# Expert stage of a two-block transformer: one gather for two experts, later transposes, one product for the remainders of gate and up

## The chip, the core and the metric

The kernel runs on one core of a Trainium2 chip. Its time is the device time of one execution in microseconds (us), the median over runs. A core has a matrix engine (TensorE; PE for its products, PEld for its weight loads), a vector engine (VectorE, DVE), an activation engine (ScalarE, ACT), GpSimd (POOL) and SyncE (SP), which here only issues DMAs of weights. Each engine works through its own queue in order and waits on semaphores for the others. Products go to PSUM, which has eight banks of 512 float32 columns; VectorE and ScalarE copy them from there.

## The reference, cut to what matters

The model has two blocks. The first is a convolution layer with a dense feed-forward, then an attention layer with a mixture of experts; the second has two more layers of other kinds. The change touches the mixture of experts alone: 256 tokens of width 1024, eight experts with a hidden width FF of 2816, and every token goes to its two best experts.

```python
logits = (h @ router_w + router_b).astype(jnp.float32)
top_vals, top_idx = lax.top_k(logits, TOP_K)
top_p = jax.nn.softmax(top_vals, axis=-1)
gates = jnp.sum(jax.nn.one_hot(top_idx, N_EXPERTS, dtype=jnp.float32) * top_p[..., None], axis=-2)
out = jnp.zeros_like(h)
for e in range(N_EXPERTS):
    out = out + gates[..., e:e + 1] * swiglu(h, w_gate[e], w_up[e], w_down[e])
```

Here swiglu(h, g, u, d) is (silu(h @ g) * (h @ u)) @ d. All inputs are float32, and the weights of one expert are 3 x 1024 x 2816 numbers, 34.6 MB.

## The kernel before, in words

Products in near float32 precision are made of three: each operand is split into a high part, rounded to the type float32r, and the rest as a low part, and `mm3` (L178) multiplies high by high, high by low and low by high into the same bank. A weight unit is 128 partitions by 1024 numbers, 512 KB. `wraw` (L129) loads it by a DMA on SyncE's queue into a raw buffer: six buffers "raw", and in the expert stage six more, "xraw", which two of five units use. `wload` (L140) splits it: ScalarE writes hi (L152), then VectorE writes lo as raw minus hi (L154). There are four hi and four lo buffers. So a unit goes through SyncE, ScalarE, VectorE and TensorE in turn.

The stage is `moe` (L853); eight PSUM banks are shared out as four "mm" (gate and up), two "sm" (gathers, transposes and the sums at the end) and two "py" (down). `experts` (L847) goes through the eight experts. Only the tokens that chose an expert are computed, up to 128 in a pass; a second pass, behind an If at the end, is for experts with more.

`gather` (L743) brings an expert's tokens together. VectorE makes a one-hot matrix of tokens by slots (L753, two instructions of 128 columns). TensorE multiplies the high and the low part of the tokens with it (L763): 8 chunks of the width, 2 parts, 2 token blocks, so 32 products of 128 columns. Four chunks fill a bank, and the four banks are copied into exh by ScalarE (L768) and exl by VectorE (L766). Then TensorE transposes the one-hot (L774) and gathers each slot's gate (L776), and VectorE copies both (oT, gs). exh, exl and oh have two buffers. The gather of expert 0 comes ahead of all experts; that of expert e + 1 is written into expert e, between its last panel and its down product (`ahead`, L823).

`expert` (L783) goes through four panels of the hidden width: 1024, 1024, 512 and 256 columns. In each panel `proj` (L793) makes the gate product (xh and xl stationary, the weights moving, at most 512 columns a product), ScalarE applies silu into h (L809), `proj` makes the up product, VectorE multiplies it into h (L814), TensorE transposes h in blocks of 128 (L819, four to a bank), ScalarE copies them as hTh (L821) and VectorE the rest as hTl (L822). The panel of 256 has 24 products of 256 columns for gate and 24 for up. The down product then has 22 units of 6 products (py). At the end ScalarE and VectorE scale it by the gate (yh, yl), TensorE brings it back to token order with oT (L842, L843), and VectorE adds it to xt (L844).

The program's text is not quite the order of the queues: when the kernel is built, a scheduler orders each engine's instructions by their place in the text and by when it estimates their inputs to be there. So products of the next panel can stand ahead of transposes that are written before them.

Of the kernel before, what the change touches and what calls it, by code (L numbers as in the profile page):

```python
# [7 lines left out]
F32 = mybir.dt.float32  # L8
F32R = mybir.dt.float32r
# [3 lines left out]
ALU = mybir.AluOpType  # L13
# [3 lines left out]
P = 128  # L17
# [25 lines left out]
class K:  # L43
# [21 lines left out]
    def psum(self, name, **cfg):  # L65
        """PSUM of a phase: banks a tag; each stream of work has its own"""
        assert sum(cfg.values()) <= 8
        self.cfg = dict(cfg)
        return self.tc.tile_pool(name=name, bufs=1, space=PSUM, reuse_waits="tile")
# [25 lines left out]
    def load_vecs(self, psp, groups, eng):  # L95
        """per-feature vectors as columns: V[:, vidx[name] + i] holds elements 128 i .. 128 i + 127"""
# [32 lines left out]
    def wraw(self, src, a, b, pool=None):  # L129
# [7 lines left out]
        self.nc.sync.dma_start(raw[:, :a * b].rearrange("p (a b) -> p a b", a=a), src)  # L137
        return raw
# [18 lines left out]
    def hold(self, ins, n):  # L157
        """the low halves of the next n units wait their turn behind ins"""
        self.held = [ins, n]
# [24 lines left out]
    def ws(self, psp, W, c0, ncol, xs, kc, kper, evac, tag="mm", pre=None):  # L184
        """out fm: chunk pairs [P, 2, 256] per bank; evac(ps, i) for pair i"""
# [16 lines left out]
    def ws32(self, psp, W, c0s, x, evac):  # L202
        """256 columns from each of c0s on, out fm, in whole float32 products; evac(pss, h) when the half h is done"""
# [15 lines left out]
    def tsteps(self, psp, W, c0, ncol, xs, kc, kper, evac, tag="mm", tail=1, pre=None, k0=0):  # L219
        """a step a group of units; out tm: [P tok, ncol] per token block; evac(ps, blk); block 0 is ahead by the last tail units; chunks from k0  # L220
        on first"""
# [21 lines left out]
    def narrow(self, pool, psp, W, c0, n, xs, fn, tag):  # L243
        """n < 128 columns of xs @ W: fn(ps, blk) with ps [P tok, n]"""
# [10 lines left out]
    def grouped(self, units, n, tail):  # L255
        """single units, the last tail of the n in one group"""
# [9 lines left out]
    def newton(self, pool, v, n, tag="nw", y=None):  # L266
        """(v) ** -0.5 on a [P, n] tile"""
# [18 lines left out]
    def bcast_rows(self, ps, col, b):  # L286
        """ps[:, P] <- col ([P,1], one value a token) laid along the free dim of all partitions"""
        self.nc.tensor.matmul(ps, col.to_broadcast([P, P]), self.ident, start=True, stop=True, skip_group_check=True)

    def stats(self, pool, psp, xf, kc=KC, div=D):  # L290
        """rstd of an fm tile: columns [P, 2] and rows [P, 256]"""
# [42 lines left out]
    def to_fm(self, psp, xt, fn, tag="tr"):  # L334
        """xt tm [P, 2, 1024]; fn(ps, c) with ps [P, 2, 256] holding chunks c, c+1"""
# [17 lines left out]
    def conv(self, psp, filler):  # L353
        nc, tc, I = self.nc, self.tc, self.I
        W = I["conv_w_in"][0]
        with tc.tile_pool(name="cv", bufs=1, reuse_waits="tile") as pool:
# [31 lines left out]
            for j in range(4):  # L388
# [14 lines left out]
                if j == 0:  # L403
                    # whole float32 products where the splits would be waited for
# [37 lines left out]
                else:  # L442
                    # squares of the first three pairs about their own mean m0, which leaves them a sum of zero
# [18 lines left out]
                    # columns: sum and sum of squares about m0  # L462
# [9 lines left out]
            # layer norm over channels: (x - m0 - d) * r, d and r by columns, then by rows  # L472
# [68 lines left out]
    def softcols(self, pool, lg):  # L541
        """log(1 + exp(-|lg|))"""
# [7 lines left out]
    def fattn(self, psp, xf, ox):  # L550
        """x2 fm -> x3 tm (written into ox [P, 2, 1024])"""
        nc, tc, I = self.nc, self.tc, self.I
        with tc.tile_pool(name="fa", bufs=1, reuse_waits="tile") as pool:
# [14 lines left out]
            # cumulative log sigmoid F, with its sign as softmax takes it, laid along the keys of every head  # L568
# [12 lines left out]
            # columns: queries 0..127 on keys 0..127, queries 128..255 on keys 0..255; -(F_q - F_k) up to F_q, which  # L581
            # is the same for all the keys of a row and leaves the softmax as it is
# [70 lines left out]
    def router(self, psp, xt, st):  # L653
        """xt: x3 tm [P, 2, D]; fills st with h3 hi / lo (tm), one-hot slots and gates"""
        nc, tc, I = self.nc, self.tc, self.I
        pers = st["pool"]
        with tc.tile_pool(name="rt", bufs=1, reuse_waits="tile") as pool:
# [43 lines left out]
            for i in range(2):  # L701
# [5 lines left out]
                if i == 0:  # L707
                    # the chosen one leaves the range of any finite logit
# [961 lines left out]
```

## Time and profile before

| | |
|---|---|
| median of 3 runs | 2069.69 us (2066.9 to 2072.44) |
| the profiled execution, first to last instruction | 2068.7 us |
| TensorE products busy | 2008.7 us (97%), 12347 products |
| VectorE busy | 1501.9 us (73%) |
| ScalarE busy | 1259.1 us (61%) |
| mean granted TensorE clock | 0.987 |
| DMA, share of 16 engines (SyncE's queue) | 64.2%, 451.07 MB |

The profile is one execution, taken by the hardware. Busy time of TensorE is modelled at the ends of products, which overlap; two starts in the timeline give the real distance. L with a number is the line of the kernel that made an instruction, and an arrow out<-in gives its tiles. Idle time of an engine is put down to what ended it.

### The profile page before, as it was taken

Reading aid. Unit: us, or ns where it says so; the run is one execution under the profiler, and the core shown is the slowest. Engines: PE = TensorE matmul, PEld = TensorE weight load, DVE = VectorE, ACT = ScalarE, POOL = GpSimd, SP = SyncE. Lnnn points to the kernel's source line nnn. Section 1 sums busy time; section 2 is a strip of 40 time slices with the busy share of each in tenths; the row PEclk is TensorE's granted clock in tenths of the full one; section 3 lists DMA queues with packets and bytes.
Section 4 is the critical chain, followed back from the end, with each engine's and each line's share of the span. In section 5 each row is a group of like instructions: output and inputs, shape, how many; then the busy total and the mean of one; then the engine's idle time right before and its main releaser. Section 6 shows DMA issues by size and latency. Waiting matters only on the chain. (4 is left out here: it accounts for less than half of the span.)

```text
span 2068.7 us, 32399 instructions
## 1 busy us (share of the span) xinstructions
PE 2008.7 (97%) x12347; PEld 1771.2 (86%) x12347; DVE 1501.9 (73%) x2089; ACT 1259.1 (61%) x1705; POOL 123.7 (6%) x236
## 2 busy tenths in 40 slices
PE   7989999999999999999999999899999999999998
PEld 7879999988888888888888888799889988888986
DVE  5976664656889898898988888776256646657644
ACT  5654444554878786777777777665444534655543
POOL 7530000100000000000000000010000000110000
PEclk9989999999999999999999999999999999999999
DMA  5325655635999898999898999543126654345552
GB/s 188 97 61 169 184 184 164 215 112 185 331 331 368 319 371 299 352 332 358 327 360 324 364 330 353 201 146 110 32 82 184 184 189 144 95 133 162 185 178 97
DMA packets 218322, 455.08 MB, mean 220 GB/s; under 512 B 17865, under 2 KB 109186, under 8 KB 218160
## 3 DMA queue, kind: packets, MB, share of 16 engines
q1 hardware_dynamic: 215536, 451.07, 64.2%
q8 instruction: 98, 1.61, 0.3%
q10 hardware_dynamic: 2112, 1.64, 0.3%
q14 instruction: 64, 0.52, 0.1%
q0 software_dynamic: 512, 0.24, 0.0%
HBM read 451.83 MB, written 1.06 MB: 219 GB/s over the span
## 5 line engine op out<-in xcount | busy, mean ns | idle before, releaser
L154 DVE TENSOR_TENSOR lo<-raw,hi 128x1024 fp32r<-128x1024 f32 x633 | 764.8, 1220 | 306.6 <-ACT hi L152 301.9
L152 ACT ACTIVATE hi<-raw 128x1024 fp32r<-128x1024 f32 x633 | 665.1, 1057 | 491.4 <-PE mm L181 248.2
L180 PE MATMUL mm<-xs,hi 128*128 128x256 f32 (+1 forms) x1488 | 427.0, 287 | 6.1 <-ACT xs L497 3.0
L181 PE MATMUL mm<-xs,hi 128*128 128x256 f32 (+1 forms) x1488 | 426.8, 287 | 3.1 <-DVE xs L327 3.1
L182 PE MATMUL mm<-xs,lo 128*128 128x256 f32 (+1 forms) x1488 | 426.6, 287 | 1.8 <-DVE lo L154 1.8
L180 PEld LDWEIGHTS mm<-xs,hi 128*128 128x128 f32 (+1 forms) x1488 | 286.9, 193 | 8.7 <-issue 4.2
L181 PEld LDWEIGHTS mm<-xs,hi 128*128 128x128 f32 (+1 forms) x1488 | 286.8, 193 | 5.3 <-DVE xs L327 4.0
L182 PEld LDWEIGHTS mm<-xs,lo 128*128 128x128 f32 (+1 forms) x1488 | 286.3, 193 | 5.2 <-issue 2.4
L181 PE MATMUL mm<-lo,exh 128*128 128x512 f32 (+1 forms) x768 | 288.5, 376 | 0.3
L182 PE MATMUL mm<-hi,exl 128*128 128x512 f32 (+1 forms) x768 | 286.7, 373 | 0.0
L180 PE MATMUL mm<-hi,exh 128*128 128x512 f32 (+1 forms) x768 | 278.0, 373 | 0.0
L154 DVE TENSOR_TENSOR lo<-xraw,hi 128x1024 fp32r<-128x1024 f32 x211 | 254.3, 1221 | 25.0 <-ACT hi L152 21.1
L152 ACT ACTIVATE hi<-xraw 128x1024 fp32r<-128x1024 f32 x211 | 221.9, 1060 | 56.7 <-PE py L182 28.4
L181 PEld LDWEIGHTS mm<-lo,exh 128*128 128x128 f32 x768 | 144.5, 188 | 29.3 <-DVE lo L154 2.7
L180 PEld LDWEIGHTS mm<-hi,exh 128*128 128x128 f32 x768 | 144.6, 188 | 25.2
L182 PEld LDWEIGHTS mm<-hi,exl 128*128 128x128 f32 x768 | 144.6, 188 | 23.2
L182 PE MATMUL py<-hi,hTl 128*128 128x512 f32 x352 | 140.5, 399 | 0.0
L181 PE MATMUL py<-lo,hTh 128*128 128x512 f32 x352 | 140.1, 398 | 0.0
L180 PE MATMUL py<-hi,hTh 128*128 128x512 f32 x352 | 137.6, 400 | 0.0
L182 PE MATMUL mm<-hi,hl 128*128 128x512 f32 x256 | 101.2, 395 | 0.0
L181 PE MATMUL mm<-lo,hh 128*128 128x512 f32 x256 | 101.1, 395 | 0.0
L180 PE MATMUL mm<-hi,hh 128*128 128x512 f32 x256 | 100.9, 395 | 0.0
(563 smaller groups left out, 2841.2 us busy)
## 6 DMA issues: line engine op xcount, KB each, us to landing
raw<-in_moe_w_up_dram SPq DMA_DIRECT2D x107, 512.0 KB, 5.4
raw<-in_moe_w_down_dram SPq DMA_DIRECT2D x107, 512.0 KB, 5.3
raw<-in_moe_w_gate_dram SPq DMA_DIRECT2D x103, 512.0 KB, 5.8
xraw<-in_moe_w_gate_dram SPq DMA_DIRECT2D x73, 512.0 KB, 7.0
xraw<-in_moe_w_up_dram SPq DMA_DIRECT2D x69, 512.0 KB, 7.3
xraw<-in_moe_w_down_dram SPq DMA_DIRECT2D x69, 512.0 KB, 6.9
raw<-in_w_up_dram SPq DMA_DIRECT2D x64, 512.0 KB, 3.7
raw<-in_w_down_dram SPq DMA_DIRECT2D x64, 512.0 KB, 3.3
```

Source lines behind the costliest of these rows:

```text
L152: nc.scalar.activation(hi[:, s:e], raw[:, s:e], AF.Copy)
L154: nc.vector.tensor_sub(lo[:, s:e], raw[:, s:e], hi[:, s:e].bitcast(F32))
L180: nc.tensor.matmul(out, lh, rh, start=first and startok, stop=False, skip_group_check=True)
L181: nc.tensor.matmul(out, lh, rl, start=False, stop=False, skip_group_check=True)
L182: nc.tensor.matmul(out, ll, rh, start=False, stop=last, skip_group_check=True)
```

## The change

One gather now makes the tokens of two experts, e and e + 1 with e even: the one-hots of both stand side by side, and each of the 32 products has 256 columns. Two chunks fill a bank, so there are eight copies in place of four, of the same size. Four transposes of one-hots fill a bank of their own, and the gates of the slots go into another. exh, exl and oh now have one buffer, of twice the size. The first pair is gathered ahead of all experts, and the next pair is gathered in the odd experts 1, 3 and 5, at the same place as before.

In `expert`, the transposes of a panel (`turned`) are written behind the gate product of the next panel. Those of the 512 panel come behind the remainder's product and those of the remainder behind the first two units of the down product. The remainder panels of gate and up are one product (`both`): `wraw2` loads a unit as two DMAs, 256 columns of gate and 256 of up side by side, and each product has 512 columns. ScalarE's silu takes the first half of the bank and VectorE multiplies by the second.

Elsewhere the diff takes out comments and docstrings only; these parts are left out here, as are blank lines.

```diff
@@ -135,6 +135,17 @@
         else:
             raw = self.t(self.rawp, [P, UNIT], "raw")
         self.nc.sync.dma_start(raw[:, :a * b].rearrange("p (a b) -> p a b", a=a), src)
+        return raw
+    def wraw2(self, srcs):
+        self.nw += 1
+        if self.xraw is not None and self.nw % 5 < 2:
+            raw = self.t(self.xraw, [P, UNIT], "xraw", bufs=6)
+        else:
+            raw = self.t(self.rawp, [P, UNIT], "raw")
+        for i, src in enumerate(srcs):
+            self.nc.sync.dma_start(raw.rearrange("p (k i n) -> p k i n", i=2, n=256)[:, :, i], src)
         return raw
     def wload(self, src, a, b, raw=None, pool=None):
@@ -741,77 +752,83 @@
                            allow_small_or_imprecise_dtypes=True)
     def gather(self, psp, pool, st, e, base):
-        """tokens in slots base..base+127 of expert e, feature-major; the one-hot transposed and the gate of a slot"""
-        nc, I = self.nc, self.I
-        hh, hl = st["hh"], st["hl"]
-        oh = self.t(pool, [P, 2, P], "oh", F32R, bufs=2)
+        nc = self.nc
+        oh = self.t(pool, [P, 2, 2, P], "oh", F32R)
         pos = st["pos"]
         if base:
             pos = self.t(pool, [P, 2, NE], "posb", bufs=2)
             nc.vector.tensor_scalar(pos, st["pos"], -float(base), None, op0=ALU.add)
         for b in range(2):
-            nc.vector.tensor_scalar(oh[:, b], st["iot"], pos[:, b, e:e + 1], st["sel"][:, b, e:e + 1],
-                                    op0=ALU.is_equal, op1=ALU.mult)
-        # gather, feature-major
-        xh = self.t(pool, [P, KC, P], "exh", F32R, bufs=2)
-        xl = self.t(pool, [P, KC, P], "exl", F32R, bufs=2)
-        for src, dst, eng in ((hh, xh, 0), (hl, xl, 1)):
-            for c4 in range(0, KC, 4):
-                ps = self.p(psp, [P, 4, P], "sm")
-                for c in range(4):
+            for i in range(2):
+                nc.vector.tensor_scalar(oh[:, b, i], st["iot"], pos[:, b, e + i:e + i + 1],
+                                        st["sel"][:, b, e + i:e + i + 1], op0=ALU.is_equal, op1=ALU.mult)
+        xh = self.t(pool, [P, KC, 2, P], "exh", F32R)
+        xl = self.t(pool, [P, KC, 2, P], "exl", F32R)
+        for src, dst, eng in ((st["hh"], xh, 0), (st["hl"], xl, 1)):
+            for c2 in range(0, KC, 2):
+                ps = self.p(psp, [P, 2, 2, P], "sm")
+                for c in range(2):
                     for b in range(2):
-                        nc.tensor.matmul(ps[:, c], src[:, b, (c4 + c) * P:(c4 + c + 1) * P], oh[:, b], start=b == 0,
+                        nc.tensor.matmul(ps[:, c], src[:, b, (c2 + c) * P:(c2 + c + 1) * P], oh[:, b], start=b == 0,
                                          stop=b == 1, skip_group_check=True)
                 if eng:
-                    nc.vector.tensor_copy(dst[:, c4:c4 + 4], ps)
+                    nc.vector.tensor_copy(dst[:, c2:c2 + 2], ps)
                 else:
-                    nc.scalar.activation(dst[:, c4:c4 + 4], ps, AF.Copy)
-        # one-hot transposed and the gate of every slot
-        oT = self.t(pool, [P, 2, P], "oT", F32R, bufs=2)
+                    nc.scalar.activation(dst[:, c2:c2 + 2], ps, AF.Copy)
+        oT = self.t(pool, [P, 2, 2, P], "oT", F32R, bufs=2)
+        pg = self.p(psp, [P, 2, 2, P], "sm")
+        ohf = oh.bitcast(F32)
+        for i in range(2):
+            for b in range(2):
+                nc.tensor.transpose(pg[:, i, b], ohf[:, b, i], self.ident)
+        nc.vector.tensor_copy(oT, pg)
         pg = self.p(psp, [P, 512], "sm")
-        ohf = oh.bitcast(F32)
-        for b in range(2):
-            nc.tensor.transpose(pg[:, b * P:b * P + P], ohf[:, b], self.ident)
-        for b in range(2):
-            nc.tensor.matmul(pg[:, 2 * P:2 * P + 1], ohf[:, b], st["gates"][:, b, e:e + 1], start=b == 0, stop=b == 1,
-                             skip_group_check=True)
-        nc.vector.tensor_copy(oT, pg[:, :2 * P].rearrange("p (b t) -> p b t", b=2))
-        gs = self.t(pool, [P, 1], "gs", bufs=2)
-        nc.vector.tensor_copy(gs, pg[:, 2 * P:2 * P + 1])
+        for i in range(2):
+            for b in range(2):
+                nc.tensor.matmul(pg[:, i:i + 1], ohf[:, b, i], st["gates"][:, b, e + i:e + i + 1], start=b == 0,
+                                 stop=b == 1, skip_group_check=True)
+        gs = self.t(pool, [P, 2], "gs", bufs=2)
+        nc.vector.tensor_copy(gs, pg[:, :2])
         return xh, xl, oT, gs
-    def expert(self, psp, pool, xt, st, e, base, got, ahead=None):
-        """adds gate * swiglu of the gathered tokens to xt; what ahead() emits runs before the last product"""
+    def expert(self, psp, pool, xt, st, e, got, ahead=None):
         nc, I = self.nc, self.I
         xh, xl, oT, gs = got
-        # gate, up
+        xh, xl, oT, gs = xh[:, :, e % 2], xl[:, :, e % 2], oT[:, e % 2], gs[:, e % 2:e % 2 + 1]
+        Wg, Wu = I["moe_w_gate"][0, e], I["moe_w_up"][0, e]
         hTh = self.t(pool, [P, FF // P, P], "hTh", F32R, bufs=1)
         hTl = self.t(pool, [P, FF // P, P], "hTl", F32R, bufs=1)
         py = [self.p(psp, [P, 512], "py") for _ in range(2)]
-        panels = [(0, 1024), (1024, 1024), (2048, 512), (2560, 256)]
         def proj(W, c0, n):
             pss = [self.p(psp, [P, 512], "mm") for _ in range(-(-n // 512))]
             for k, m, (wh, wl) in self.wunits(W, c0, n, KC, UNIT // n):
                 for kk in range(m):
                     for i, p in enumerate(pss):
-                        w = min(512, n - 512 * i)
-                        s = slice(512 * i, 512 * i + w)
-                        self.mm3(p[:, :w], xh[:, k + kk], xl[:, k + kk], wh[:, kk, s], wl[:, kk, s], k + kk == 0,
+                        s = slice(512 * i, 512 * i + 512)
+                        self.mm3(p, xh[:, k + kk], xl[:, k + kk], wh[:, kk, s], wl[:, kk, s], k + kk == 0,
                                  k + kk == KC - 1)
             return pss
-        hts = []
-        for c0, n in panels:
-            pg_ = proj(I["moe_w_gate"][0, e], c0, n)
-            h = self.t(pool, [P, 1024], "h", bufs=2)
-            for i, p in enumerate(pg_):
-                w = min(512, n - 512 * i)
-                nc.scalar.activation(h[:, 512 * i:512 * i + w], p[:, :w], AF.Silu)
-            pu_ = proj(I["moe_w_up"][0, e], c0, n)
-            for i, p in enumerate(pu_):
-                w = min(512, n - 512 * i)
-                d = h[:, 512 * i:512 * i + w]
-                nc.vector.tensor_mul(d, p[:, :w], d)
+        def both(c0):
+            ps = self.p(psp, [P, 512], "mm")
+            for k in range(0, KC, 2):
+                raw = self.wraw2([W[k * P:(k + 2) * P, c0:c0 + 256].rearrange("(k p) n -> p k n", p=P)
+                                  for W in (Wg, Wu)])
+                wh, wl = self.wload(None, 2, 512, raw)
+                for kk in range(2):
+                    self.mm3(ps, xh[:, k + kk], xl[:, k + kk], wh[:, kk], wl[:, kk], k + kk == 0, k + kk == KC - 1)
+            return ps
+        def turned(h, c0, n):
             for i in range(0, n // P, 4):
                 m = min(4, n // P - i)
                 ps = self.p(psp, [P, 4, P], "sm")
@@ -847,11 +886,11 @@
     def experts(self, psp, pool, xt, st, base):
         got = self.gather(psp, pool, st, 0, base)
         for e in range(NE):
-            ahead = (lambda: self.gather(psp, pool, st, e + 1, base)) if e + 1 < NE else None
-            got = self.expert(psp, pool, xt, st, e, base, got, ahead)
+            ahead = (lambda: self.gather(psp, pool, st, e + 1, base)) if e % 2 and e + 1 < NE else None
+            got = self.expert(psp, pool, xt, st, e, got, ahead) or got
     def moe(self, xt, st, ahead, gf, rc):
-        """x3 tm -> x4 tm, in place"""
         nc, tc = self.nc, self.tc
         with self.psum("pse", mm=4, sm=2, py=2) as psp, \
                 tc.tile_pool(name="ex", bufs=1, reuse_waits="tile") as pool, \
```

## Rows read from the trace of the kernel before

**Rows 1.** Busy time by stretch, expert 5: us, busy us (instructions) an engine, PEclk, DMA share, GB/s.
```profile
1019.70:1120.70 101.00, 100.84 (x489) 82.97 (x488) 89.94 (x89) 76.22 (x83) 0.00 (x0) 1.00 0.93 343
```

**Rows 2.** Waits, 520 to 1320 us: who <- for whom: us in total, times, longest.
```profile
ACT hi L152 <- PE py L182: 73.2, 156, 4.3
...
PEld sm L819 <- DVE h L814: 5.3, 21, 0.3
```

**Rows 3.** Waits of SyncE's weight queue, 520 to 1300 us.
```profile
SPq L137 <- DVE lo L154: 534.2, 302, 7.0
```

**Rows 4.** Groups by shape, 580 to 1320 us: xcount | busy us, mean ns | idle before.
```profile
L154 DVE TENSOR_TENSOR lo<-raw,hi 128x1024 fp32r<-128x1024 f32 x289 | 346.8, 1221 | 33.8 <-ACT hi L152 31.4 <-DMA xraw<-in_moe_w_down_dram 0.3
...
L766 DVE CAST exl<-sm 128x512 fp32r<-128x512 f32 x14 | 9.6, 688 | 3.9 <-PE sm L763 3.4
L768 ACT ACTIVATE exh<-sm 128x512 fp32r<-128x512 f32 x14 | 8.2, 594 | 4.4 <-PE sm L763 4.4
```

**Rows 5.** Timeline of PE around a gather: start us, us, instruction xcount [idle before].
```profile
1086.70 1.09 PE L763 MATMUL sm<-oh,h3h 128*128 128x128 f32 x8
1087.62 0.44 PE L180 MATMUL py<-hi,hTh 128*128 128x512 f32 x1
...
1088.60 0.40 PE L181 MATMUL py<-lo,hTh 128*128 128x512 f32 x1
1089.11 1.11 PE L763 MATMUL sm<-oh,h3h 128*128 128x128 f32 x8
1090.05 1.96 PE L763 MATMUL sm<-oh,h3l 128*128 128x128 f32 x16
1091.98 0.44 PE L774 MATMUL sm<-ident,oh 128*128 128x128 f32 x2
...
1092.62 0.48 PE L182 MATMUL py<-hi,hTl 128*128 128x512 f32 x1
```

**Rows 6.** Timeline of PE around the third gather in the loop.
```profile
780.98 2.29 PE L763 MATMUL sm<-oh,h3h 128*128 128x128 f32 x16
784.07 2.00 PE L763 MATMUL sm<-oh,h3l 128*128 128x128 f32 x16 [0.81 <-ACT exh L768]
...
787.16 0.77 PE L180 MATMUL py<-hi,hTh 128*128 128x512 f32 x1
```

**Rows 7.** Timeline of PE around a remainder panel.
```profile
1076.06 0.39 PE L180 MATMUL mm<-hi,exh 128*128 128x512 f32 x1
...
1079.46 0.28 PE L180 MATMUL mm<-hi,exh 128*128 128x256 f32 x1
...
1080.41 0.66 PE L819 MATMUL sm<-ident,h 128*128 128x128 f32 x4
1080.82 0.36 PE L181 MATMUL mm<-lo,exh 128*128 128x256 f32 x1
...
1085.83 0.40 PE L180 MATMUL py<-hi,hTh 128*128 128x512 f32 x1
```

**Rows 8.** Timeline of all engines around the gather of expert 0.
```profile
509.30 0.59 DVE L753 TENSOR_SCALAR oh<-iot,pos,sel 128x128 fp32r<-128x128 f32 x2
...
509.79 2.12 PE L763 MATMUL sm<-oh,h3h 128*128 128x128 f32 x16
...
515.39 0.48 PE L180 MATMUL mm<-hi,exh 128*128 128x512 f32 x1
```

**Rows 9.** DMA issues of the page: xcount, KB each, median us to landing.
```profile
raw<-in_moe_w_up_dram SPq DMA_DIRECT2D x107, 512.0 KB, 5.4
```

**Rows 10.** Timeline of PE at a panel's transposes.
```profile
1044.44 0.39 PE L180 MATMUL mm<-hi,exh 128*128 128x512 f32 x1
1044.70 0.66 PE L819 MATMUL sm<-ident,h 128*128 128x128 f32 x4
```

**Rows 11.** Busy time by stretch, the stretch with the fullest DMA engines.
```profile
640.00:665.00 25.00, 25.00 (x116) 20.64 (x115) 23.53 (x24) 20.72 (x22) 0.00 (x0) 1.00 1.02 367
```

**Rows 12.** Busy time by stretch, behind the third gather in the loop.
```profile
786.00:793.00 7.00, 7.00 (x21) 5.77 (x21) 3.44 (x7) 2.11 (x2) 0.00 (x0) 0.52 0.44 148
```

More of the change, by code (lines that the diff above doesn't have):

```diff
@@ L822, in expert @@
                 nc.vector.tensor_sub(hTl[:, f:f + m], ps[:, :m], hTh[:, f:f + m].bitcast(F32))
+        late = None
+        for c0, n in ((0, 1024), (1024, 1024), (2048, 512)):
+            pg_ = proj(Wg, c0, n)
+            h = self.t(pool, [P, 1024], "h", bufs=2)
+            for i, p in enumerate(pg_):
+                nc.scalar.activation(h[:, 512 * i:512 * i + 512], p, AF.Silu)
+            if late is not None:
+                turned(*late)
+            pu_ = proj(Wu, c0, n)
+            for i, p in enumerate(pu_):
+                d = h[:, 512 * i:512 * i + 512]
+                nc.vector.tensor_mul(d, p, d)
+            late = (h, c0, n)
+        ps = both(2560)
+        h = self.t(pool, [P, 1024], "h", bufs=2)
+        nc.scalar.activation(h[:, :256], ps[:, :256], AF.Silu)
+        nc.vector.tensor_mul(h[:, :256], ps[:, 256:], h[:, :256])
+        turned(*late)
+        late = (h, 2560, 256)
         nxt = ahead() if ahead is not None else None
@@ L826, in expert @@
         for k, m, (wh, wl) in self.wunits(I["moe_w_down"][0, e], 0, D, nf, 1):
-            for kk in range(m):
-                for i in range(2):
-                    s = slice(512 * i, 512 * i + 512)
-                    self.mm3(py[i], hTh[:, k + kk], hTl[:, k + kk], wh[:, kk, s], wl[:, kk, s], k + kk == 0,
-                             k + kk == nf - 1)
+            for i in range(2):
+                s = slice(512 * i, 512 * i + 512)
+                self.mm3(py[i], hTh[:, k], hTl[:, k], wh[:, 0, s], wl[:, 0, s], k == 0, k == nf - 1)
+            if k == 1:
+                turned(*late)
         yh = self.t(pool, [P, D], "yh", F32R, bufs=2)
```

## The prediction

> **What bounds the kernel now.** I read the page's slices first, for the stage: the eight experts, one after another, are some 800 of 2068.7 us, in which TensorE and the DMA engines are both near full. Then busy time by stretch, one stretch an expert: in the 101.0 us of expert 5 TensorE is busy 100.84, VectorE 89.94, ScalarE 76.22, and the DMA engines hold a share of 0.93 [rows 1]. Since matmul ends are modelled, I did not trust "busy" and asked who waits for whom: ScalarE's split of a weight unit (hi) waits 73.2 us in 156 places for TensorE to free a buffer, while the longest wait on TensorE's side, that of its weight loads for the product h, is 5.3 us in all [rows 2]. The weight queue of SyncE waits 534.2 us for VectorE to free a raw buffer [rows 3]. So the back-pressure runs from TensorE to ScalarE, VectorE and SyncE: what shortens TensorE's list in this stage shortens the kernel, until another engine catches up. Last I read the PE timeline start to start, which does not depend on modelled ends, for the price of each kind of product.
>
> **Gather.** Before, each of the experts 1 to 7 has a gather, which lies between its predecessor's last panel and down product; two copies of each kind in every one make 14 and 14 [rows 4]. A usual one: 8 products in 0.92 us (1086.70 to 1087.62), 24 in 2.87 (1089.11 to 1091.98), so 3.79 us for 32, 0.118 each; transposes and gate columns 0.64 (to 1092.62); and 0.28 of waiting: of the five py products between, four take 0.98 us (1087.62 to 1088.60) and the fifth 0.23, as 512-wide ones do elsewhere [rows 7], so 1.21 of the 1.49 us to 1089.11 [rows 5]. Sum 4.71 us. Six are like that one. The one at 780.98 had no py products between its copies and took 6.18 us, to 787.16 [rows 6]. Together 6 x 4.71 + 6.18 = 34.4 us.
>
> After, three gathers lie in the loop, for two experts each. A gather has 32 products again, now 256 columns wide. No row shows a 256-wide gather; the nearest are the 256-wide products of the remainder panel, 41 in 5.01 us, 0.122 each [rows 7]. Bounds: 0.118 (width costs nothing) to 0.236 (proportional to width); I take 0.120, as moving 256 float32r columns behind a 128x128 weight load is just what those rows do: 3.84 us. Four transposes and eight gate columns: twice 0.64 = 1.28. Eight bank copies in place of four still go through two "sm" banks, so waits can be more than 0.28: from 0 to the rival below, I take 1.0. Sum 6.1 us, three times 18.3. Saved: 34.4 - 18.3 = 16.1 us.
>
> **First gather.** It lies bare on the path: 509.79 to 515.39, 5.6 us [rows 8], and expert 0 cannot begin before it ends. It now makes two experts' tokens. VectorE's two one-hot instructions, 0.59 us from 509.30 on, release its first product, and now there are four [rows 8]. Lower bound: the one-hots (0.6), transposes and columns (0.64) and 0.2 us for width, +1.4. Upper bound: all of it twice, +6.2. It is bound by copies, not products, so I take two ScalarE copies of 0.594 and two VectorE copies of 0.688 more [rows 4], 2.6, beside the one-hots and the 0.64: +3.8.
>
> **Remainder.** 48 products of 256 columns run from 1079.46 to 1085.83, 6.37 us, of which the transposes between them take 0.41: 5.96. In one 512-wide product there are 24, at 0.2267 (15 products from 1076.06 to 1079.46 take 3.40) [rows 7], so 5.44. That is 0.5 us an expert; 0.1 of it is the disturbance by the transposes, which moves with them. I take 0.4, times 8: 3.2 us. The splits stay four units of 1024 elements; the products h of the panel stay one activation and one multiplication. Four units an expert now take two issues on SP of 256 KB each; SP waits two thirds of the stage [rows 3], so four more issues an expert are covered. The Trainium skill (DMA: Bandwidth & Descriptors, Measured) speaks against smaller transfers: it asks for a MiB or more, and its fit, made on transfers that GpSimd issued, gives each about 2 us of fixed cost. Taken as serial, an estimate by that page is 2 us more on 32 units, 64 us, and the kernel would be slower. Here a 512 KB transfer lands 5.4 us after its issue [rows 9], and an expert's 66 come in 101 us [rows 1], so they overlap and latency is not paid one after another; I give that rule nothing in the sum.
>
> **Transposes.** The trace already has them behind the first product of the next panel, not ahead of it: at 1044.70, 0.26 us after a product that starts at 1044.44, where 0.227 is usual [rows 10]. What a later place can save is that 0.03 us in some 40 groups, 1 us, and the wait of 5.3 us is that of a weight load that is already covered. I take 1.0 (bounds 0 and 3, as VectorE's hTl subtractions move from a panel's start, where its multiplications lie, to its middle). The remainder's two go behind two down units and are needed 18 units later.
>
> **What is late next.** An expert without a gather falls from 101.0 to 101.0 - 4.71 - 0.4 = 95.9 us. VectorE has 89.94 us in one [rows 1], of which the gather's part now lies in every second expert: free. The weights, 34.6 MB, at 367 GB/s (the fullest stretch) [rows 11] need 94.3 us: free, but near. A gather pair in an odd expert gives 6 us back. Nearer limits mean small new waits; between 0 and 10 us, I take 0.25 us an expert, 2.0 in all.
>
> **Sum.** 16.1 + 3.2 + 1.0 - 3.8 - 2.0 = 14.5 us. The profiled execution spans 2068.7 us, 1.0 under the median of the runs, 2069.69: 2054.2 by the profile, 2055.2 beside the median.
>
> **Rivals.**
> (a) *The copies of the pair's gather queue behind splits; slower.* The gather at 780.98 took 1.5 us more than the others: its first 16 products needed 2.29 us, and the next ones, at 784.07, had waited 0.81 us for ScalarE's copy [rows 6], which stood behind splits. Then TensorE's granted clock was 0.52 from 786 to 793, nearly all of it at 1.2 GHz in place of 2.4, a loss of 7 x 0.48 = 3.4 us [rows 12]. Eight copies through two banks have more places for that. The Trainium skill (TensorE: Matmul & The Clock Gate, A second HAM failure mode) tells the same of PSUM banks cycled in each iteration: short idle times between groups of products let the clock swing; by that each of the three gathers would cost a stretch like the one at 786, which is the case priced here. If each copy stands behind one split (VectorE's 1.22 us taken for both engines [rows 4]), eight take 5.1 + 9.8 = 14.9 us, a gather 16.2, three 48.6: 14.2 over before. With 6.2 more ahead of expert 0, two more slow stretches 6.8, less 4.2 for remainder and transposes: +23.0, 2093. It decides from where a pair's gather takes over (34.4 + 3.2 + 1.0 - 3.8 - 2.0) / 3 = 10.9 us. Against it: only one gather of seven shows it, in four like [rows 5] py products stand between the copies, and four hi and lo buffers let few splits pile up.
> (b) *The weight stream becomes the bound.* The stretch with 367 GB/s has a share of 1.02 [rows 11]; at 1.00 it would be 360 GB/s, 96.1 us an expert, 0.2 over TensorE's 95.9, and in a long gather the 12 buffers fill and the stream stops for 2 us or so. Five experts without a gather, and three pauses: some 8 us of the gain lost, 2063. For it: VectorE frees buffers in bunches. Against: SP still waits for buffers, not for engines [rows 3].
> (c) *The wide gather costs by its columns*, so the change does not do there what it says: 64 x 0.12 = 7.7 us in place of 3.84, three times 3.9 = 11.7 lost, 2067. The remainder's rows speak against it.
> (d) *More than I count*: no slow stretch after a gather (3.4), no new waits (2.0), the first gather at its lower bound (2.4): 2047.4.
>
> **How the numbers follow.** Forecast 0.63 (its own range 2049 to 2062), (a) 0.09, (b) 0.13, (c) 0.04, (d) 0.11. Predicted: 2055.2. The range goes from under (d), 2046, over (b) and (c) to 2068; outside it is most of (a). What can be told from no change is 0.3%, 6.2 us: faster means under 2063.5. Forecast, (d) and the better half of (b) are there: 0.81. Same: the rest of (b), (c), and the lightest of (a): 0.11. Slower: 0.08.
>
> **What would show it.** Right: three gathers in the loop, each 5 to 7 us start to start with 256-wide products at 0.12; experts 0, 2, 4, 6 and 7 near 96 us from first product to last and 1, 3 and 5 near 101; remainder near 5.5 us; the first gather near 9 us; TensorE still without holes, and SP still waiting mostly for VectorE. Wrong: gathers over 11 us or a clock near 0.5 after each (a); ScalarE's splits waiting for DMA in place of TensorE (b); products of the gather 0.2 us apart (c).

## The result and the profile after

The changed kernel takes 2085.88 us, median of 4 runs (2080.08 to 2088.2), against 2069.88 of the kernel before beside it (4 runs): a ratio of 1.0071, 95% interval 1.0054 to 1.0089. Slower by 0.7%, where 2055.2 was forecast, in a range of 2046 to 2068. The profiled execution spans 2085.0 us against 2068.7, and all of the 16 us are in the expert stage: from the first gather product to the last product of the last scatter it takes 828.6 us in place of 812.7.

The busy time of an expert without a gather (719.5 to 820.5) and of one with (820.5 to 928.0), in the columns of [rows 1]:

```profile
719.50:820.50 101.00, 97.84 (x427) 77.14 (x426) 88.34 (x85) 73.73 (x81) 0.00 (x0) 1.00 0.91 338
820.50:928.00 107.50, 104.36 (x471) 83.30 (x470) 92.74 (x95) 75.92 (x85) 0.00 (x0) 0.98 0.91 323
```

The forecast was 96 and 101. TensorE, busy 100.84 of 101.00 us before, now has 3.2 us of holes in each of the two, and VectorE and the DMA engines are no busier than they were (VectorE 88.34 and 92.74 us, the second with a pair's gather, for 89.94 [rows 1]). So it is not a limit that was reached, but waiting. Waits by who waited for whom, 520 to 1337 us (us in total, times, longest), after:

```profile
ACT hi L163 <- PE mm L193: 61.9, 139, 3.7
...
PEld mm L192 <- DVE lo L165: 35.2, 40, 2.4
ACT h L848 <- PE mm L193: 25.9, 15, 2.8
ACT yh L875 <- PE py L193: 20.4, 8, 2.7
```

and three of them in the kernel before (520 to 1320):

```profile
ACT h L809 <- PE mm L182: 12.3, 21, 1.0
...
PEld mm L181 <- DVE lo L154: 2.7, 6, 0.5
...
ACT yh L836 <- PE py L182: 1.7, 1, 1.7
```

TensorE's weight loads wait 35.2 us for VectorE's part of a weight split (lo); before it was 2.7. ScalarE's yh, the evacuation of an expert's result, stands at the head of its queue some 2.6 us too early at all eight ends (20.4 in eight); before at one. ScalarE's silu (h) waits 25.9 us in three of the four gate panels, where all four had 12.3 before. ScalarE's hi waited for a transfer for less than half a microsecond in all, and SyncE still waits for VectorE [rows 3], so the weights are there:

```profile
SPq L137 <- DVE lo L165: 493.4, 271, 9.4
```

The gathers themselves did what was forecast, and more. TensorE's timeline around the first one in the loop (start us, us, instruction, count) answers to [rows 5]:

```profile
678.05 0.63 PE L775 MATMUL sm<-oh,h3h 128*128 128x256 f32 x4
678.52 0.40 PE L192 MATMUL mm<-lo,exh 128*128 128x512 f32 x1
...
681.07 1.10 PE L775 MATMUL sm<-oh,h3h 128*128 128x256 f32 x8
682.01 0.39 PE L192 MATMUL py<-lo,hTh 128*128 128x512 f32 x1
```

Eight products of 256 columns take 0.94 us (681.07 to 682.01), 0.118 each, just what the 128-wide ones took. Other products stand between the groups, so the copies cost next to nothing, and the gather's own instructions take 5.03 us, start to start.

Where does TensorE stop? At the end of an expert (924 to 931 us), VectorE after:

```profile
921.08 1.22 DVE L165 TENSOR_TENSOR lo<-raw,hi 128x1024 fp32r<-128x1024 f32 x1 [0.18 <-ACT hi L163]
924.43 1.41 DVE L876 SCALAR_TENSOR_TENSOR yl<-py,gs,yh 128x512 fp32r<-128x512 f32 x2 [2.13 <-ACT yh L875]
926.26 2.91 DVE L883 TENSOR_TENSOR x<-sm,x 128x512 f32<-128x512 f32 x4 [0.42 <-PE sm L882]
929.09 2.35 DVE L165 TENSOR_TENSOR lo<-raw,hi 128x1024 fp32r<-128x1024 f32 x2
```

TensorE after:

```profile
928.04 0.40 PE L882 MATMUL sm<-yl,oT 128*128 128x512 f32 x1
930.36 0.50 PE L192 MATMUL mm<-lo,exh 128*128 128x512 f32 x1 [1.92 <-DVE lo L165]
```

and VectorE at such an end before:

```profile
1020.49 1.23 DVE L154 TENSOR_TENSOR lo<-xraw,hi 128x1024 fp32r<-128x1024 f32 x1 [0.17 <-ACT hi L152]
1021.63 1.41 DVE L837 SCALAR_TENSOR_TENSOR yl<-py,gs,yh 128x512 fp32r<-128x512 f32 x2
1023.01 1.39 DVE L844 TENSOR_TENSOR x<-sm,x 128x512 f32<-128x512 f32 x2
1024.32 1.21 DVE L154 TENSOR_TENSOR lo<-xraw,hi 128x1024 fp32r<-128x1024 f32 x1
1025.45 1.28 DVE L844 TENSOR_TENSOR x<-sm,x 128x512 f32<-128x512 f32 x2
```

Before, three units of the next expert are split ahead of yh and yl, and the fourth stands between the additions to x. After, one unit is: yl waits 2.13 us at the head of VectorE's queue with splits behind it, the four additions stand together, and the second unit's lo starts at 929.09. TensorE has nothing to multiply from 928.27 (a product's 0.23 us after the start at 928.04) to 930.36.

The same happens inside an expert. ScalarE after, around the end of the second gate panel:

```profile
748.17 2.95 ACT L163 ACTIVATE hi<-raw 128x1024 fp32r<-128x1024 f32 x3
753.90 1.09 ACT L848 ACTIVATE h<-mm 128x512 f32<-128x512 f32 x2 [2.77 <-PE mm L193]
754.87 2.00 ACT L163 ACTIVATE hi<-xraw 128x1024 fp32r<-128x1024 f32 x2
```

TensorE after:

```profile
755.98 0.73 PE L191 MATMUL mm<-hi,exh 128*128 128x512 f32 x2 [0.31 <-ACT hi L163]
757.24 0.50 PE L192 MATMUL mm<-lo,exh 128*128 128x512 f32 x1 [0.52 <-DVE lo L165]
```

and ScalarE at such a place before:

```profile
1055.90 1.28 ACT L809 ACTIVATE h<-mm 128x512 f32<-128x512 f32 x2 [0.98 <-PE mm L182]
1057.08 1.05 ACT L152 ACTIVATE hi<-raw 128x1024 fp32r<-128x1024 f32 x1
```

After, silu (L848) waits 2.77 us for the panel's last product, with all but one of the next panel's splits behind it; TensorE then starts two products 0.46 and 0.69 us late. Before, two units stand ahead of silu here, it waits 0.98 us, and TensorE does not stop. The two places recur: 2.08 us at each of seven ends, 14.5 in all, and 1.15 us behind the second gate panel of seven experts, 8.0 in all.

### The profile page after: what moved, and what is told of

Its sections match the earlier page's. It is cut to its first block, busy times and chain, and to the rows that moved or that the text cites. A ratio compares the mean times of both kernels' runs of the same rounds, so it can differ in the third digit from the quotient of the medians.

```text
span 2085.0 us, 31801 instructions
## 1 busy us (share of the span) xinstructions
PE 2005.1 (96%) x12027; PEld 1744.2 (84%) x12027; DVE 1505.0 (72%) x2081; ACT 1248.1 (60%) x1705; POOL 121.5 (6%) x236
## 5 line engine op out<-in xcount | busy, mean ns | idle before, releaser
L192 PE MATMUL mm<-lo,exh 128*128 128x512 f32 x704 | 282.2, 401 | 19.9 <-DVE lo L165 19.2
L193 PE MATMUL mm<-hi,exl 128*128 128x512 f32 x704 | 276.1, 392 | 0.0
L165 DVE TENSOR_TENSOR lo<-xraw,hi 128x1024 fp32r<-128x1024 f32 x211 | 253.5, 1221 | 25.9 <-ACT hi L163 23.4
L191 PE MATMUL mm<-hi,exh 128*128 128x512 f32 x704 | 257.4, 395 | 2.1 <-ACT hi L163 2.1
L163 ACT ACTIVATE hi<-xraw 128x1024 fp32r<-128x1024 f32 x211 | 219.8, 1060 | 45.3 <-PE mm L193 25.9
L192 PEld LDWEIGHTS mm<-lo,exh 128*128 128x128 f32 x704 | 133.0, 189 | 63.1 <-DVE lo L165 35.2
L191 PEld LDWEIGHTS mm<-hi,exh 128*128 128x128 f32 x704 | 132.2, 189 | 34.7 <-ACT hi L163 7.3
L193 PEld LDWEIGHTS mm<-hi,exl 128*128 128x128 f32 x704 | 133.1, 189 | 24.9
L191 PE MATMUL py<-hi,hTh 128*128 128x512 f32 x352 | 123.4, 397 | 0.0
```

The lines of the kernel that those rows point to most:

```text
L163: nc.scalar.activation(hi[:, s:e], raw[:, s:e], AF.Copy)
L165: nc.vector.tensor_sub(lo[:, s:e], raw[:, s:e], hi[:, s:e].bitcast(F32))
L191: nc.tensor.matmul(out, lh, rh, start=first and startok, stop=False, skip_group_check=True)
L192: nc.tensor.matmul(out, lh, rl, start=False, stop=False, skip_group_check=True)
L193: nc.tensor.matmul(out, ll, rh, start=False, stop=last, skip_group_check=True)
```

## The experiments

In this table "stage" runs from the first gather product to the last scatter product of the profiled execution, start to start; "waits" is what TensorE's starts come later than 0.235 us after the start of a 512-wide product ahead of them, summed over the stage outside stretches at half clock (good to about 1 us); "half clock" is the time lost to a granted clock of 0.5 (1.2 GHz in place of 2.4), from the clock's own record; "gather" is the gathers' own time, start to start, outside such stretches. The median and the ratio are of all runs, the ratio against the kernel before on the same chip. The four other columns are of one execution, which can lie some us off the median: 6.3 us above it in e1, 6.0 below it in e8 and 4.6 below it in e7.

| kernel | median us | ratio, 95% interval | stage | waits | half clock | gather |
|---|---|---|---|---|---|---|
| before | 2069.9 | 1 | 812.7 | 8.8 | 3.4 | 36.8 |
| changed | 2085.9 | 1.0071 (1.0054 to 1.0089) | 828.6 | 42.3 | 3.4 | 21.5 |
| e1 pair's gather alone | 2075.5 | 1.0031 (1.0019 to 1.0043) | 821.2 | 30.6 | 5.1 | 21.9 |
| e2 late transposes alone | 2088.4 | 1.0090 (1.0076 to 1.0104) | 827.2 | 18.8 | 5.1 | 40.6 |
| e3 one remainder product alone | 2092.2 | 1.0109 (1.0093 to 1.0125) | 835.1 | 13.9 | 20.5 | 36.4 |
| e4 changed, yh and yl behind three splits | 2085.0 | 1.0082 (1.0068 to 1.0096) | 829.9 | 40.3 | 8.5 | 21.6 |
| e5 = e1, order written out | 2052.5 | 0.9909 (0.9892 to 0.9926) | 794.3 | 9.4 | 0 | 21.8 |
| e6 = changed, order written out | 2057.3 | 0.9938 (0.9922 to 0.9954) | 799.0 | 16.9 | 0 | 21.6 |
| e7 = e5 and the remainder | 2051.7 | 0.9918 (0.9901 to 0.9935) | 795.3 | 14.0 | 0 | 22.0 |
| e8 before, yh behind one split | 2079.9 | 1.0056 (1.0035 to 1.0076) | 820.6 | 17.4 | 3.4 | 36.0 |
| e9 = e3, gather spread | 2077.1 | 1.0038 (1.0024 to 1.0052) | 818.3 | 18.9 | 1.7 | 38.8 |
| e10 = e5 without silu's order | 2058.3 | 0.9948 (0.9932 to 0.9963) | 799.7 | 14.3 | 0 | 21.9 |
| e11 = e2, transposes mid panel | 2072.5 | 1.0015 (1.0005 to 1.0026) | 814.3 | 12.2 | 0 | 37.0 |
| e12 = e6, transposes mid panel | 2055.0 | 0.9931 (0.9917 to 0.9944) | 797.1 | 15.7 | 0 | 21.9 |

**e1 to e3: each part alone.** Each is the kernel before with one part of the change.

```diff
 e1, with gather() as in the change
-            ahead = (lambda: self.gather(psp, pool, st, e + 1, base)) if e + 1 < NE else None
+            ahead = (lambda: self.gather(psp, pool, st, e + 1, base)) if e % 2 and e + 1 < NE else None
 e2
+            if late is not None:
+                turned(*late)
             pu_ = proj(Wu, c0, n)
...
-            turned(h, c0, n)
+            late = (h, c0, n)
 e3
-        panels = [(0, 1024), (1024, 1024), (2048, 512), (2560, 256)]
+        panels = [(0, 1024), (1024, 1024), (2048, 512)]
...
+        ps = both(2560)
```

> The kernel before with the pair's gather alone (remainders and transposes as before). Theory T1, order of the queues: with the pair's gather the next expert's first weight splits stand behind yh and yl in ScalarE's and VectorE's queues (one unit of the next expert is split ahead of yh, three in the kernel before), so TensorE waits for splits behind every scatter and again in the panels: gathers -16.1 + 3.8, waits +25 to +32, in all 2083 to 2090, and the waits of TensorE name lo (VectorE). Rival R1, the late transposes block ScalarE's queue: this kernel has none, so it has the gather's gain alone, about 2058. Rival R2, the remainder's 512-wide product with two transfers to a unit delays the weights: as R1, about 2058. Rival R3, the weights' transfers bound the stage once the gathers are short: 2080 to 2090 too, but ScalarE's hi waits for raw data (a DMA) and not only for TensorE.

> The kernel before with the late transposes alone. T1: 2067 to 2070 (0 to -3 against before), since yh and yl stand behind three splits of the next expert as before. R1: slower by 15 to 30, 2085 to 2100. R2, R3: no change.

> The kernel before with the remainders of gate and up in one product alone. T1: -3, 2067. R2: slower by 15 or more, 2085. R1, R3: about -3.

Every part alone made the kernel slower. T1 was right on the sign of e1, not on its size (+6.4 us for the 14 to 21 expected), and wrong on e2 and e3; no rival had all three either. The table shows why "one cause" was the wrong question. In e1 the gathers are 14.9 us shorter and the waits 21.8 longer. In e2 the waits are 10.0 longer and the gathers 3.8. In e3 it is the clock, 17.1 us more than before. What they share is that the order of the engines' queues differs from the kernel before, in part in places that the edit does not touch: yh and yl in e1, the gathers in e2 and e3. In e2 the edit itself puts hTh next to silu: hTh waits 2.60 us for its transposes at the head of ScalarE's queue. ScalarE of e2:

```profile
1057.16 0.60 ACT L837 ACTIVATE hTh<-sm 128x512 fp32r<-128x512 f32 x1 [2.60 <-PE sm L835]
1057.65 1.05 ACT L164 ACTIVATE hi<-raw 128x1024 fp32r<-128x1024 f32 x1
1059.24 1.09 ACT L849 ACTIVATE h<-mm 128x512 f32<-128x512 f32 x2 [0.54 <-PE mm L194]
1060.22 0.60 ACT L837 ACTIVATE hTh<-sm 128x512 fp32r<-128x512 f32 x1
1060.69 2.02 ACT L164 ACTIVATE hi<-raw 128x1024 fp32r<-128x1024 f32 x2
```

One unit is split between 1057.16 and 1060.69; TensorE uses one in 1.36 us (six products of 0.227 [rows 7]) and stops twice:

```profile
1061.82 0.73 PE L192 MATMUL mm<-hi,exh 128*128 128x512 f32 x2 [0.53 <-ACT hi L164]
1063.07 0.50 PE L193 MATMUL mm<-lo,exh 128*128 128x512 f32 x1 [0.53 <-DVE lo L166]
```

In e3 the gather has become one piece. TensorE of e3, and its busy time behind it:

```profile
1099.70 2.29 PE L775 MATMUL sm<-oh,h3h 128*128 128x128 f32 x16
1102.79 2.53 PE L775 MATMUL sm<-oh,h3l 128*128 128x128 f32 x16 [0.81 <-ACT exh L780]
...
1106.27 0.77 PE L193 MATMUL py<-lo,hTh 128*128 128x512 f32 x1
```

```profile
1104.00:1111.00 7.00, 7.00 (x25) 6.02 (x24) 3.04 (x5) 1.99 (x2) 0.00 (x0) 0.51 0.42 163
```

It is [rows 6] and [rows 12] over again: 38 small products with a wait of 0.81 us for a copy inside, and then a granted clock of 0.51. Here such a stretch begins near the end of seven of the eight gathers, five of 6.8 us and two of 3.4, 20.5 us lost in all, where the kernel before has one of 6.8 us.

**e4: only yh and yl behind the splits.**

```diff
+        if e + 1 < NE:
+            nxt_w = self.wsrc(I["moe_w_gate"][0, e + 1], 0, 1024, KC, 1)
+            self.pre = [self.wload(src, m, 1024) for _, (k, m, src) in zip(range(3), nxt_w)] + [None] * 5
         for i in range(2):
-            nc.scalar.activation(yh[:, s], py[i], AF.Copy, scale=gs)
+            with self.tc.issue_after(self.hins):
+                nc.scalar.activation(yh[:, s], py[i], AF.Copy, scale=gs)
```

(and yl behind the third lo in the same way)

> The changed kernel with one more thing: the first three weight units of the next expert are split ahead of yh and yl in the two queues, as they stand in the kernel before; transfers, arithmetic and the rest as in the changed kernel. T1: the wait behind the scatter goes (some 2.1 us an expert at seven ends, and the waits of yl and of the additions with it, 15 to 20 in all), 2066 to 2071, and more if the waits in the panels were its echo (2055); if they have an order of their own, they stay. R1: the wait in the panels stays and the end's goes, 2070. R2, R3 (weights late in any order): as the changed kernel, 2086.

No gain, and T1's range is missed by 14 us: by the time alone R3 would have won. VectorE's timeline tells otherwise:

```profile
922.64 1.40 DVE L902 SCALAR_TENSOR_TENSOR yl<-py,gs,yh 128x512 fp32r<-128x512 f32 x2
926.40 2.90 DVE L909 TENSOR_TENSOR x<-sm,x 128x512 f32<-128x512 f32 x4 [2.35 <-PE sm L908]
929.21 2.35 DVE L169 TENSOR_TENSOR lo<-xraw,hi 128x1024 fp32r<-128x1024 f32 x2
```

yl no longer waits, but the four additions stand next in the queue, TensorE now does the scatter behind the products of the split units, and VectorE waits 2.35 us for it. The wait behind the scatter is again 1.92 us. One waiting instruction was moved; the next one took its place. (In the table the waits fall by 2.0 us, and 5.1 us more at half clock take that back.)

**e5 to e7: the order of all three queues.** At the end of an expert and behind a gate panel the order of the kernel before is written out. For silu it is the order of its first three experts, three units ahead; from expert 3 on, the kernel before has two at the second panel. The comments in this cut and in the next two are added here.

```diff
+        self.pre = [self.wload(w, m, 1024) for m, w in src[:3]]      # next expert's units 0 to 2
...
+            with self.tc.issue_after(self.hins) if more else nullcontext():
                 nc.scalar.activation(yh[:, s], py[i], AF.Copy, scale=gs)
...
+            if b and more:
+                self.pre.append(self.wload(w, m, 1024))              # unit 3, between the additions
...
+                with self.tc.issue_after(self.lins) if b and more and 1 else nullcontext():
                     nc.vector.tensor_add(xt[:, b, s], ps, xt[:, b, s])
...
+                        if sc and k < 2:                             # scatter between units 0 and 1
+                            self.mm3s(sc[6 * k + 3 * i:], *a)
...
+            if n == 1024:                                            # three up units, then silu
+                pre = [self.wload(src, m, n) for _, (k, m, src) in zip(range(3), self.wsrc(Wu, c0, n, KC, 1))] + [None] * 5
+                with self.tc.issue_after(self.hins) if pre else nullcontext():
                     nc.scalar.activation(h[:, 512 * i:512 * i + w], p[:, :w], AF.Silu)
```

> The pair's gather alone, with the order of the kernel before written out at the end of an expert and behind the gate panels: three units of the next expert split ahead of yh and yl, the fourth between the second and the third addition to x, the scatter's products between those of the next expert's first two units, and three units of the up panel split ahead of silu. Theory T1, now for all the queues (a wait moves to the next instruction that stands ahead of a split, as the additions did when only yh was moved): the waits for lo go, the gathers' 12 us stay won: 2055 to 2060 against 2068.6. Rival R3, the splits or the weights are late in any order: 2075, as the pair's gather alone. Rival R4, half the clock behind the gathers costs the difference: 2070, with the halves of the clock still there.

> The changed kernel with the same order written out. T1: 2054 to 2062. R3: 2085, as the changed kernel. R4: 2080.

> The pair's gather and the one product for the remainders, with transposes as before and the order written out. T1: e5 less the remainder's 3 us, 2052 to 2057. If the remainder's two transfers to a unit or its order cost by themselves (R2): e5 or slower, 2060 to 2080.

All three came out as T1 said, e6 inside its range, e5 2.5 us and e7 0.3 us under theirs. Arithmetic and transfers of e6 are those of the changed kernel; only order differs, and it is 28.6 us faster. Two experts of e5, without and with a gather, and its waits for lo:

```profile
715.90:812.30 96.40, 96.33 (x451) 78.78 (x450) 88.13 (x85) 75.17 (x80) 0.00 (x0) 1.00 0.97 360
812.30:913.90 101.60, 101.53 (x496) 83.89 (x495) 92.33 (x95) 77.32 (x84) 0.00 (x0) 1.00 0.95 340
```

```profile
PEld mm L201 <- DVE lo L168: 6.1, 15, 0.5
```

96.4 and 101.6 us, the forecast's 95.9 and 101, with TensorE busy throughout. R3 falls: at 360 GB/s the weights keep up. R4 falls as the main cause: e5's stage is 26.9 us shorter than that of e1, 21.2 of it by waits and 5.1 by the clock, whose halves are gone. e5 and e7 have the lowest times here and can't be told apart.

**e8: the kernel before, with yh early.**

```diff
+            hy = nc.scalar.activation(yh[:, s], py[i], AF.Copy, scale=gs).ins
...
+        if e + 1 < NE:
+            self.ynext = (hy, ly)      # hi and lo of the next expert's unit 1 issue behind these
```

> The kernel before with one thing of the changed kernel's order: yh and yl stand behind one split of the next expert in place of three. T1: a wait of about 2 us behind the scatter at seven ends, 2080 to 2086. R3: no change, 2069. R4: no change by this, other than what it does to the clock.

Slower, as T1 had it, at the lower end: TensorE's waits grow by 8.6 us, 1.2 an end in place of 2, since here the second unit's lo is still between the additions.

**e9: e3 with the gather spread.**

```diff
+                if between is not None and not eng and c4 == 0:
+                    last = between(g)      # six products of the down projection
...
+                with self.tc.issue_after(last) if last is not None else nullcontext():
                     for c in range(4):     # the other gather products
```

> The one product for the remainders alone (e3) with one change: six products of the down projection stand between the first eight and the other gather products, as five of them do in the kernel before. Theory T2: e3 lost its time because its gathers ran in one piece of 38 small products with a wait of 1 us for exh inside, and the granted clock fell to half behind four of them (6.8 us each, 20.5 us of clock lost in the stage against 6.8 before); here the halves go and the time is 2064 to 2072. Rival R2, the remainder's product or its two transfers to a unit cost it: no change against e3, 2088 to 2093.

The halves behind those four gathers are gone and 15.1 us with them, so T2 holds for the clock (the kernel before loses 3.4 us to it and not 6.8, which is how long its stretch lasts). One stretch of 3.4 us is left in e9's stage, behind the third gather in the loop. The time stays 5 us above its range, on a wait that T2 did not have. TensorE of e9:

```profile
987.37 0.40 PE L194 MATMUL mm<-hi,exl 128*128 128x512 f32 x1
988.95 0.44 PE L839 MATMUL sm<-ident,h 128*128 128x128 f32 x2 [1.18 <-DVE h L870]
989.14 1.09 PE L777 MATMUL sm<-oh,h3h 128*128 128x128 f32 x8
990.06 0.44 PE L192 MATMUL py<-hi,hTh 128*128 128x512 f32 x1
```

The remainder's transposes follow its last product at once and wait 1.18 us for silu and the multiplication, which now both come at the very end of the product; "waits" in the table has 11.1 us of this kind.

**e10: e5 without silu's order.** The block under `if n == 1024` is left out.

```diff
-            if n == 1024:
-                pre = [self.wload(src, m, n) for _, (k, m, src) in zip(range(3), self.wsrc(Wu, c0, n, KC, 1))] + [None] * 5
```

> The pair's gather with the order written out at the end of an expert alone; silu stands behind one or two splits of the up panel, as in the pair's gather alone, where e5 has three. T1: between e1 and e5: the waits behind the scatter gone, those behind the second gate panel (about 0.8 us an expert) there, 2056 to 2062. If the panels' waits were only an echo of the end's: as e5, 2052.

Inside T1's range, 5.9 us slower than e5, with 4.9 us more of waits: the panel's waits have an order of their own and are not an echo of the end's.

**e11 and e12: transposes in the middle of the up panel.**

```diff
+                if late is not None and k + m == KC // 2:
+                    with self.tc.issue_after(last):
+                        turned(*late)
             return pss
...
-            if late is not None:
-                turned(*late)
-                late = None
-            pu_ = proj(Wu, c0, n)
+            pu_ = proj(Wu, c0, n, late)
```

> The late transposes alone (e2), put in the middle of the up panel in place of its start, so that hTh and hTl stand three to four splits behind silu and not next to it. T1: e2's waits for hi and lo in the panels (1.9 us an expert) go, what its gathers and the clock cost stays: 2070 to 2077. Rival: the clock and the gathers are all of e2's loss: no change, 2085 to 2090.

> All three parts with the order written out (e6), and the transposes in the middle of the next up panel. T1, with the forecast's 1.0 us for the transposes: 2050 to 2054, the best of all. If late transposes give nothing by themselves: 2052 to 2057, no better than e7 without them.

e11 is inside T1's range and 15.9 us faster than e2: its waits fall by 6.6, and its gathers, which shifted too, by 3.6, and the clock stays up; it is still slower than before by 0.15%, so late transposes gain nothing here. e12 says so for the whole: between e6 and e7, to be told from neither, and no better than e7 without them.

## Why the prediction was wrong

The step that failed is "What is late next": "Nearer limits mean small new waits; between 0 and 10 us, I take 0.25 us an expert, 2.0 in all." The waits grew from 8.8 to 42.3 us, 33.5 in place of 2.0. The forecast looked at the engines' loads, found room on each, and took the order of their queues as given; the runs showed that the order had changed, with yh and yl behind one split unit of the next expert in place of three and silu behind one at the second gate panel, and that 28.6 us go when the order is written out (e6). A lead, units split before TensorE needs them, comes back slowly once it is lost: VectorE starts a lo every 1.13 us when nothing holds it (two in 2.35 us at 929.09, one in 1.22) and TensorE uses a unit in 1.36, an estimate of at most 0.23 us a unit, 1.8 over the eight units to the next evacuation, where a lead of three units is worth 4.1. The lead was the kernel's asset, and no load shows it.

Point by point:
- *Gather.* Forecast 16.1 us saved in the loop, 3.8 lost at the first: 12.3. Measured 15.3 for both together (36.8 to 21.5): 16.2 saved in the loop, as forecast, and only 0.9 more for the first gather's own instructions, since other products stand between the copies there too, where expert 0's own products start before the gather ends. The price in the loop was 5.0 us a gather and not 6.1. Rival (c) is out with 0.118 us a product.
- *Remainder.* The forecast's 0.4 us an expert was too much: in e7 the panel takes 5.80 us without its transposes (864.48 to 870.69 less 0.41) against 5.96 [rows 7], 0.16 or 1.3 us in all in place of 3.2, and against e5 2.6 us more of waits in the down projection took that. e5 and e7 can't be told apart.
- *Transposes.* The 1.0 us is not there, and in the changed kernel they are hardly late: TensorE does the first panel's at 743.72, eight products into the next gate projection and not behind its 48, a place like that of [rows 10], and the second panel's seven products into the next. There the change did not do what it says.
- *Sum.* Stage: -15.3 for the gathers, -1.6 for the remainder (its eight panels 47.4 to 45.8), 0 for the clock, +33.5 for waits: +16.6, measured +15.9. With the order written out all three parts come to 2057.3 (e6), near the forecast, which is luck, on errors that offset: gathers 2.9 and the clock 3.4 better than its terms, waits 6 worse, the remainder and the transposes some 2.5 worse.
- *Rivals.* (b) is out: hi does not wait for transfers, and e5 runs at 360 GB/s. (a) priced the right thing at the wrong place: a gather whose copies stand behind splits, and a clock at 0.5 behind it, is what made e3 slow, and not the pair's gather. By the Trainium skill (TensorE: Matmul & The Clock Gate, A second HAM failure mode) short idle times between groups of products make the clock swing; the trace agrees for gathers in one piece with a wait of 0.81 us inside (0.51 behind that at 1099.70 of e3), and shows no such stretch behind the three pairs' gathers of the changed kernel, whose two, of 3.4 us each, come with two of the seven holes of 2 us at the ends of experts (822.7 and 1239.1).
- *What would show it* had the right tests: "TensorE still without holes" and the experts near 96 and 101 us failed (101.0 and 107.5), and the gathers, the first gather at 9 us (509.45 to 518.83) and SyncE's waits held.

What stays open: why the scheduler that orders the queues put yh, silu and hTh earlier in these kernels. All kernels here with the pair's gather have yh behind one split unless told otherwise, and all without it behind three unless told otherwise; its reasons show in no trace, and no run tried them.

## What to carry to other kernels

Where one queue holds both the run-ahead work of a pipeline and the evacuations that must wait for its end, the number of run-ahead units ahead of each evacuation is a quantity to read from the timeline before a change and to read again after it. A faster neighbour may shift it, and then the change is judged by an order that it was not about: pin the order, and measure again. When one blocking instruction is moved and nothing is gained, look at the next one in the same queue before giving up the cause.

## What the runs showed of the chip

Gather products of 256 float32r columns start 0.118 us apart, as 128-wide ones do (0.118 [rows 5]), so a second expert's tokens cost TensorE's gather products nothing there. A gather of 38 small products in one piece, with a wait near 0.8 us inside, ended in a granted clock of 0.5, for 6.8 us at a time in four of e3's experts and for 3.4 us in a fifth; six 512-wide products between its groups (e9) left the clock at 1.00 in those four, though waits of 0.9 to 1.2 us stood just ahead. One piece alone is not enough: e11 has all its gathers in one piece or with one other product in it, with waits of at most 0.36 us inside, and a clock of 1.00 throughout the stage. Nor is it the only case: e2 has three stretches of 3.4 us in or right behind gathers with eleven other products between.
